# Attention of a hybrid layer on one core: the maxima row, the query copies, the first weights, the values and the last sums written in other places

## The chip, the cores and the metric

The kernel runs on one core of a Trainium2 chip. The metric is the device time of one execution in microseconds (us). A core has TensorE (PE in the profile, with its weight loads as PEld), VectorE (DVE), ScalarE (ACT), GpSimd (POOL) and SyncE (SP). SP computes nothing here: it issues most DMA transfers, strictly in its own order, and POOL issues some too.

## The reference, cut to what matters

One layer: a combined input projection feeds an RWKV-7 branch (A) and a latent attention branch (B), both are gated, projected, merged by sigmoid gates, projected again and added to the input. The change lies in branch B and at its two ends. Branch B computes, for 8 heads and 2048 tokens:

```
q = (rmsnorm(c_q, g_q) @ w_uq)       # per head 64 plain + 32 rotary
kv = (rmsnorm(c_kv, g_kv) @ w_ukv)   # per head 64 key + 64 value
q_pe = rope(q_pe, cos, sin);  k_pe = rope(k_pe, cos, sin)     # k_pe is shared by the heads
s = (q_nope . k_nope + q_pe . k_pe) * scale, masked to key <= query
p = softmax(s);  o = p @ v;  y_b = (o * silu(z_b)) @ w_out_b
```

## The kernel before

Every fp32 operand of a matrix product is split into a high and a low part, and a product is made as three matmuls (`mm3`). The time falls into three stretches. **Phase 1** (to about 1138 us) makes the input projections, the RWKV chunks, the values of the attention and, last, gate projections (tile `pj`) that are stored for the output phase (`d_zg`). Then comes a **seam**: the weights of the first pair of heads, its keys, the first queries. **Phase 2** (to about 1803 us) is the attention; **phase 3** makes the remaining gates, the output projections and the norm.

The attention works on pairs of heads (4 pairs `p`) and groups of 512 queries (4 groups `g`): 16 items, `i = 4p + g`. One item needs, in this order:

- `queries(i)`: two projections of six matmuls into one PSUM tile `pq`. Half k=0 holds the plain part, copied out as QH (ACT) and QL (DVE); half k=1 the rotary part, which DVE turns with the table `rt` (loaded by SP), splits as `qhl`, and which SP then copies by six DMAs of 64 KB into the tiles QR and QM.
- `row_max(i)`: for each 128 queries a tile `pm` of approximate scores, its maximum over the keys taken by DVE (`mx`, about 1.2 us for a full tile), then the negated maxima (`mh`), turned into a row by eight small matmuls (`pn`) and copied by ACT into row 32 of QM. That row is used in the fifth of the five products of a score tile, so that the exponential sees scores minus maximum.
- `attend(i)`: for each block `kb` of 128 keys a score tile `pst` (five products, each a pair of matmuls for the two heads), the exponential on ACT (`acc` for the first block, `pt` for the others), the value product into `po` and the sum of the exponentials on POOL (`acc`, 2 us a tile).

`pm`, `pq`, `pn`, `pst` and `bc` share one PSUM tag `st` with three buffers. The matmuls of the attention keep the order in which they are written; all other instructions are ordered by a scheduler. The written order comes from a list `steps`: before an item starts, its own maxima and the queries of the next item must be done (`due`); as far as that allows, `slot` puts one step between score tiles. Where an item is due and its steps are not done, they stand in a row, and I call that a forced start. At the end `total` sums `acc` over the partitions (`psum_s`), and `norm` spreads the reciprocals (`bc`) over the outputs. After that phase 3 begins with gate projections `pj`, whose weights `whl` and inputs `xh`, `xl` are loaded during the last items.

At the seam, `attn_weights(0)` loads nine small pieces of weights behind the last stores on SP (kraw and wqraw), `keys` makes pk in two halves, and the rotary keys are loaded once for all items by six transfers of 256 KB on POOL (tiles KR4 and KR5, named KR in the profile).

Of the kernel before, what the change touches and what calls it, by code (L numbers as in the profile page):

```python
# [19 lines left out]
P = 128  # L20
# [29 lines left out]
def hybrid_layer(ctx, tc, x, positions, g_pre, w_in, b_gate, mu_shift, w0, w_decay_up, a0, w_iclr_up, k_k, k_a,  # L50
# [234 lines left out]
    def proj(ps, w, X, cut=1):  # L285

        XH, XL = X
        for i in range(cut):
            t = slice(i * 512 // cut, (i + 1) * 512 // cut)
            mm3(ps[:, t], [(w[c], (XH[:, c, t], XL[:, c, t])) for c in range(KC)])  # L290


    with st:
# [590 lines left out]
        def attn_weights(p, pool, bufs):  # L884

            kraw = pool.tile([P, 2, HD], F32, name="kraw", tag="kraw", bufs=1)
# [3 lines left out]
            split(kwh, kwl, kraw.rearrange("p h n -> p (h n)"), A, V)  # L890
# [3 lines left out]
            for pieces in ([(HD * h, HD, hq[h][:, 0:HD]) for h in range(2)],  # L894
# [3 lines left out]
                qws[p].append(load_w(pool, None, 2, P, bufs=bufs, tag="wq", pieces=pieces))  # L898
# [5 lines left out]
        split(vh, vl, vraw, A, V)  # L904
        run(step(NH))
        for t in range(NT):
            ps = pp.tile([P, 512], F32, name="pv2", **(dict(tag="z", bufs=2) if t % 3 else dict(tag="e", bufs=1)))
            ts_ = slice(t * P, (t + 1) * P)
            mm3(ps, [((kvl[:, 0, ts_], kvl[:, 1, ts_]), (vh, vl))])
# [8 lines left out]
        sw = kst.enter_context(tc.tile_pool(name="pw", bufs=1, reuse_waits="tile", side="right"))  # L918
        attn_weights(0, sw, 2)
# [6 lines left out]
        def keys(p, psp, ptag, pbufs, mm):  # L926

            kwh, kwl = kws[p]
            for s in range(0, NS, 2):
# [6 lines left out]
                yield  # L936

# [17 lines left out]
        def queries(i, Q, sb, psp, ptag, pbufs, cqt=None, rt=None, mm=PE.matmul):  # L955
# [21 lines left out]
            split(hl[:, 0], hl[:, 1], ra, A, V)  # L977
            for h in range(2):
# [6 lines left out]
        def row_max(i, Q, KR4, sb, psp, ptag, pbufs, mm=PE.matmul):  # L985
# [5 lines left out]
            for j in range(4):  # L991
                js = slice(j * P, (j + 1) * P)
                for c in range(g + 1):
# [13 lines left out]
                    yield  # L1007
# [3 lines left out]
            V.tensor_scalar(mh, m1, -1.0, None, op0=ALU.mult)  # L1011
            pn = psp.tile([P, 2, 512], F32, name="pn", tag=ptag, bufs=pbufs)
            for h in range(2):
                for j in range(4):
                    mm(pn[0:1, h, j * P:(j + 1) * P], lhsT=mh[:, h, j:j + 1], rhs=identr, start=True, stop=True)
            for h in range(2):
                A.copy(QM[HD * h + 32:HD * h + 33, :], pn[0:1, h, :])
            yield
# [14 lines left out]
    with ExitStack() as st:  # L1033
# [3 lines left out]

        KR4 = sb.tile([P, T], F32R, name="KR4")
# [314 lines left out]
```

## Time and profile before

| what | us |
|---|---|
| median of three runs | 2496.98 (2496.0 to 2503.67) |
| the profiled execution | 2498.47 |
| its span in the trace | 2496.7 |
| PE busy | 2245.2 (90% of the span) |
| DVE busy | 1096.9 (44%) |
| ACT busy | 709.5 (28%) |
| POOL busy | 1018.5 (41%) |
| mean granted clock of TensorE | 0.945 |

A granted clock of 1.00 is 2.4 GHz, 0.50 is 1.2 GHz. The share of PE is an average: it is full during most of phases 1 and 3, some 87% in the attention and 41% at the seam. At the lower clock a matmul counts as busy for twice as long, so the busy share and the granted clock are read together.

### The profile page before, as it was taken

How to read it: one execution, taken by the hardware profiler on the slowest of the kernel's cores; microseconds unless marked ns; L12 is line 12 of the kernel's file. 1: busy time of each engine (PE TensorE's matmuls, PEld its weight loads, DVE VectorE, ACT ScalarE, POOL GpSimd, SP SyncE). 2: the span in 40 equal slices, each digit the busy share in tenths (PEclk: the TensorE clock that was granted, in tenths of full speed). 3: DMA queues.
4: the chain of work that ended last, by engine and by line, in shares of the span. 5: the costliest groups of instructions: out<-in, count | busy, mean ns of one | idle time of the engine just before them, and what ended most of it. 6: DMA issues, size and time to landing. Idle time of an engine off the chain costs nothing.

```text
span 2496.7 us, 37813 instructions
## 1 busy us (share of the span) xinstructions
PE 2245.2 (90%) x14313; PEld 1689.0 (68%) x14313; DVE 1096.9 (44%) x2005; ACT 709.5 (28%) x1267; POOL 1018.5 (41%) x1200
## 2 busy tenths in 40 slices
PE   7979998998999999894788989887799989999997
PEld 5656776777777777673565555554488867788776
DVE  7154785757677675422444534344130142310312
ACT  4342342333243432221233333322222211111111
POOL 7453542444275653211235654544522222312422
PEclk9989999989999999897889999999899999999999
DMA  7787766746577876745111112050197795765863
GB/s 249 217 270 231 238 218 182 204 118 210 168 222 203 259 200 228 205 136 148 55 57 56 49 56 73 28 186 7 52 358 235 268 333 208 278 211 195 322 236 118
DMA packets 314031, 454.75 MB, mean 182 GB/s; under 512 B 113661, under 2 KB 206905, under 8 KB 308025
## 3 DMA queue, kind: packets, MB, share of 16 engines
q1 hardware_dynamic: 283672, 404.09, 50.4%
q0 software_dynamic: 12896, 44.04, 5.5%
q10 hardware_dynamic: 17280, 4.20, 1.0%
q8 instruction: 113, 1.85, 0.3%
q14 instruction: 70, 0.57, 0.1%
HBM read 313.30 MB, written 132.64 MB: 179 GB/s over the span
## 4 chain that ended last, share of the span: by engine, by line
PE 64%; DVE 14%; DMA 12%; POOL 4%; issue 2%; ACT 2%; SPq 1%; ACTq 0%; POOLq 0%; DVEq 0%
PE pj L281 8%; PE pj L283 8%; PE pj L282 8%; PE pst L1066 7%; PE po L1066 5%; DMA wraw<-in_w_in_dram 3%; PE pm L1066 3%; PE pz L618 3%; DVE mx L1006 2%; DMA whl<-d_wi 2%; DVE Xg L673 2%; PE pout L281 2%; PE py L281 2%; PE pout L282 2%; PE py L283 2%
## 5 line engine op out<-in xcount | busy, mean ns | idle before, releaser
L281 PE MATMUL pj<-xh,whl 128*128 128x512 f32 (+2 forms) x1344 | 540.9, 402 | 39.0 <-DMA whl<-d_wi 26.6
L283 PE MATMUL pj<-xh,whl 128*128 128x512 f32 (+2 forms) x1344 | 537.9, 400 | 5.6 <-POOL whl L248 5.5
L282 PE MATMUL pj<-xl,whl 128*128 128x512 f32 (+2 forms) x1344 | 536.1, 399 | 0.0
L1120 POOL TENSOR_TENSOR acc<-acc,pt 128x1024 f32<-128x1024 f32 (+2 forms) x144 | 290.3, 2016 | 240.9 <-ACT pt L1107 113.8
L281 PEld LDWEIGHTS pj<-xh,whl 128*128 128x128 f32 (+1 forms) x1344 | 258.8, 193 | 105.7 <-DMA whl<-d_wi 27.3
L283 PEld LDWEIGHTS pj<-xh,whl 128*128 128x128 f32 (+1 forms) x1344 | 258.6, 192 | 69.0 <-POOL whl L248 10.8
L282 PEld LDWEIGHTS pj<-xl,whl 128*128 128x128 f32 (+1 forms) x1344 | 258.4, 192 | 55.5 <-issue 2.1
L1006 DVE TENSOR_REDUCE mx<-pm 128x2 f32<-128x1024 f32 (+3 forms) x160 | 166.7, 1062 | 215.9 <-PE pm L1066 215.3
L248 POOL TENSOR_TENSOR whl<-wraw,whl 128x512 fp32r<-128x512 f32 (+1 forms) x114 | 148.4, 1304 | 166.8 <-ACT whl L247 147.7
L1278 DVE SCALAR_TENSOR_TENSOR tg<-tg,py 128x512 f32<-128x512 f32 x64 | 43.9, 687 | 313.3 <-PE py L283 217.6
L1107 ACT ACTIVATE pt<-pst 128x1024 f32<-128x1024 f32 (+2 forms) x144 | 126.9, 883 | 187.7 <-PE pst L1066 177.7
L1280 POOL TENSOR_TENSOR tg<-tg 128x512 f32<-128x512 f32 x32 | 41.3, 1290 | 211.5 <-DVE tg L1278 211.5
L247 ACT CAST whl<-wraw 128x512 fp32r<-128x512 f32 (+1 forms) x116 | 71.4, 615 | 187.0 <-DMA wraw<-in_w_in_dram 99.1
L1066 PE MATMUL po<-pt,Vt 128*64 128x512 f32 (+3 forms) x576 | 122.3, 542 | 0.0
L281 PE MATMUL py<-BH,whl 128*128 128x512 f32 x256 | 102.5, 401 | 10.0 <-DVE tg L1278 9.9
L282 PE MATMUL py<-BL,whl 128*128 128x512 f32 x256 | 102.0, 399 | 0.0
L283 PE MATMUL py<-BH,whl 128*128 128x512 f32 x256 | 102.0, 398 | 0.0
L282 PE MATMUL pout<-wf,MH 128*128 128x512 f32 x256 | 101.0, 395 | 0.0
L283 PE MATMUL pout<-wf,ML 128*128 128x512 f32 x256 | 99.5, 395 | 0.0
L281 PE MATMUL pout<-wf,MH 128*128 128x512 f32 x256 | 97.2, 395 | 0.5 <-DMA wf<-d_wf 0.5
L671 DVE TENSOR_TENSOR tq<-Xg,Qg 128x30 f32<-128x30 f32 (+7 forms) x240 | 77.5, 323 | 44.6 <-DMA Xg<-d_q 39.1
L740 POOL TENSOR_TENSOR sp<-uv,pcs 64x256 f32<-64x256 f32 x64 | 41.1, 643 | 118.6 <-DVE uv L754 115.9
(372 smaller groups left out, 4044.1 us busy)
## 6 DMA issues: line engine op xcount, KB each, us to landing
whl<-d_wi SPq DMA_DIRECT2D x222, 512.0 KB
d_wi<-whl SPq DMA_DIRECT2D x80, 512.0 KB
wraw<-in_w_in_dram SPq DMA_DIRECT2D x98, 256.0 KB
whl<-d_wo SPq DMA_DIRECT2D x48, 512.0 KB
wf<-d_wf SPq DMA_DIRECT2D x48, 512.0 KB
cqt<-d_cq POOLq DMA_DIRECT2D x16, 1024.0 KB, 5.3
d_zg<-thg SPq DMA_DIRECT2D x42, 256.0 KB
xl<-d_x POOLq DMA_DIRECT2D x8, 1024.0 KB, 10.3
```

What stands on the lines that cost most here:

```text
L247: (ehi.copy if ehi is A else ehi.tensor_copy)(hi, src)
L248: elo.tensor_tensor(lo, src, f32(hi), op=ALU.subtract)
L281: mm(ps, lhsT=lh, rhs=rh, start=(i == 0), stop=False)
L282: mm(ps, lhsT=lh, rhs=rl, start=False, stop=False)
L283: mm(ps, lhsT=ll, rhs=rh, start=False, stop=(stop and i == n - 1))
L618: PE.matmul(pz[:, p, :], lhsT=E["BK"][p][b, c, :], rhs=E["AR"][b, p, c, :], start=True, stop=True)
L671: V.tensor_tensor(t3, Xg[:, 0:m, s_:s_ + 1].to_broadcast([P, m, n]), Qg[:, s_:s_ + 1, s_ + 1:32].to_broadcast([P, m, n]), op=ALU.mult)
L673: V.tensor_tensor(Xg[:, 0:m, s_ + 1:32], Xg[:, 0:m, s_ + 1:32], t3, op=ALU.add)
L1006: V.tensor_reduce(mx[:, :, j, c], pm[:, :, 0:w], axis=AX.X, op=ALU.max)
L1066: tc.keep_in_program_order(PE.matmul(*args, **kw))
L1107: A.activation(pt[:, :, q0:512], pst[:, :, q0:512], AF.Exp, scale=scale)
L1120: G.tensor_tensor(acc[:, :, q0:512], acc[:, :, q0:512], pt[:, :, q0:512], op=ALU.add)
```

## The change

It has six parts:

1. `attn_weights(0)` is written ahead of the last RWKV step, in memory that is free by then, and all attention weights go through one raw buffer (`raws=1`, tag wqraw shared with kraw).
2. The 16 value tiles (48 matmuls) are no longer written before the stored gates, but between the first keys, the first query projection and the first maxima, with their matmuls kept in written order.
3. The rotary keys are loaded by `rot_keys` in transfers of 64 KB on SP: first 512 tokens into a tile of its own for item 0 (6 transfers), then the whole for all other items (24 transfers).
4. `queries` projects the rotary half first (k = 1, then 0); rope and its split stand ahead of the copies QH and QL, and PE projects both halves without a stop.
5. `row_max` ends with `mh`. The row `pn` is made by `max_row` inside `attend`, after the first four products of the item's first two score tiles; the fifth products follow. The queries of the next item stand four maxima steps before the end of the list instead of three, and the first two blocks of an item have one slot for steps instead of three.
6. Three of the gate projections of phase 3 (`pj2`, 24 matmuls each) are written between the last sums.

```diff
         split(vh, vl, vraw, A, V)
+        sw = kst.enter_context(tc.tile_pool(name="pw", bufs=1, reuse_waits="tile", side="right"))
+        attn_weights(0, sw, 2)
         run(step(NH))
-        for t in range(NT):
+        def value(t):
...
+            mm3(ps, [((kvl[:, 0, ts_], kvl[:, 1, ts_]), (vh, vl))], mm=pin)
...
+        def rot_keys(pool, n):
+            K4 = pool.tile([P, n * 512], F32R, name="KR4")
+            K5 = pool.tile([P, n * 512], F32R, name="KR5")
+            for s in range(n):
+                ss_ = slice(s * 512, (s + 1) * 512)
+                for r in range(4):
+                    nc.sync.dma_start(f32(K4[32 * r:32 * r + 32, ss_]), f32(d_kr[:, 0, ss_]))
+                for h in range(2):
+                    nc.sync.dma_start(f32(K5[HD * h:HD * h + 32, ss_]), f32(d_kr[:, 1, ss_]))
...
-            for k in range(2):
-                ps = pq[:, k, :]
-                mm3(ps, [(qws[p][k][c], (cqt[:, c, 0, :], cqt[:, c, 1, :])) for c in range(2)], mm=mm)
-                if k == 0:
-                    split(QH, QL, ps, A, V)
+            for k in (1, 0):
+                mm3(pq[:, k, :], [(qws[p][k][c], (cqt[:, c, 0, :], cqt[:, c, 1, :])) for c in range(2)], mm=mm)
+            ps = pq[:, 1, :]
...
             split(hl[:, 0], hl[:, 1], ra, A, V)
+            split(QH, QL, pq[:, 0, :], A, V)
...
+        KR0 = rot_keys(sq, 1)
         with tc.tile_pool(name="pks", bufs=1, reuse_waits="tile", space=PSUM) as ppk:
-            for _ in queries(0, Q0, sq, ppk, "pk", 1, load_cq(0, sq), load_rt(0, sq)):
-                pass
+            t = 0
+            for _ in queries(0, Q0, sq, ppk, "pk", 1, load_cq(0, sq), load_rt(0, sq), mm=pin):
+                for t in range(t, t + 3):
+                    value(t)
+                t += 1
+            for _ in row_max(0, Q0, KR0[0], sq, ppk, "pk", 1, mm=pin):
+                for t in range(t, min(t + 2, NT)):
+                    value(t)
+                t += 1
...
-        KR4 = sb.tile([P, T], F32R, name="KR4")
-        KR5 = sb.tile([P, T], F32R, name="KR5")
-        for r in range(4):
-            G.dma_start(KR4[32 * r:32 * r + 32, :], d_kr[:, 0, :])
...
+        KR4, KR5 = rot_keys(sb, NS)
...
+                    for sc in two:
+                        next(sc)
+                    max_row(i, Q[i % NQ] if i else Q0, pp, "st", 3)
+                    flush(0)
+                    for sc in two:
+                        next(sc)
+                    slot(0)
...
-            at_ = max(0, len(steps) - 3)
+            at_ = max(0, len(steps) - 4)
...
-        while after:
-            follow()
+        for p in range(4):
+            if p < 3:
+                ps = pp.tile([P, 2, 512], F32, name="pj2", tag="st", bufs=3)[:, 0]
+                proj(ps, load_w(sx, w_in[:, C_ZA + p * P:C_ZA + (p + 1) * P], KC, P, elo=V, bufs=5,
+                                key=f"i{C_ZA + p * P}"), X, mm=pin)
...
+            for _ in range(1 if p < 3 else len(after)):
+                follow()
```

What this makes of the order of instructions is shown at three places. The first is the seam on SP. Before, behind the last gate store (d_zg) stand the weights and three tables; the rotary keys are on POOL's queue and not here:

```order
L492 DMA d_zg_17_401<-thg 128x512
L887 DMA kraw<-in_w_ukv_dram 128x2x64
L269 DMA wqraw<-in_w_uq_dram 128x2x64 x2
L269 DMA wqraw<-in_w_uq_dram 128x2x32
L269 DMA wqraw<-in_w_uq_dram 128x2x16 x2
L269 DMA wqraw<-in_w_uq_dram 128x2x32
L269 DMA wqraw<-in_w_uq_dram 128x2x16 x2
L945 DMA rt<-d_rope 128x512 x3
```

Now the weights are gone from here; the six copies of item 0's queries (QRx, QMx) are followed by the 24 loads of the whole rotary keys (KR_11905 and KR_11906; three more rounds of six are left out), and only then by the tables rt of items 1 and 2 and the query copies of item 1 (QR_11939). The first of the 24 loads writes memory that phase 1 held, and waits for the last value matmul:

```order
L1000 DMA QRx<-qhl 32x512
L1001 DMA QRx<-qhl 32x512
L1002 DMA QMx<-qhl 32x512
L951 DMA KR_11905<-d_kr 32x512 x4
L953 DMA KR_11906<-d_kr 32x512 x2
...
L966 DMA rt<-d_rope 128x512 x2
L891 DMA kraw<-in_w_ukv_dram 128x2x64
L966 DMA rt<-d_rope 128x512
L1000 DMA QR_11939<-qhl 32x512
```

The 24 loads moved from POOL to SP and stand between item 0's query copies and everything of item 1.

The second place is a forced start on PE, that of item 10. Before, two maxima tiles (pm) stand between the query projections (pq, twelve matmuls) and the row pn, and all five products of a score tile (pst) behind it:

```order
L1066 MATMUL pq<-cqt,wqhl 128x512 x12
L1066 MATMUL pm<-KH_11778,QH_11864 128x512 x2
L1066 MATMUL pm<-KR_11850,QR_11866 128x512 x2
L1066 MATMUL pm<-KH_11778,QH_11864 128x512 x2
L1066 MATMUL pm<-KR_11850,QR_11866 128x512 x2
L1066 MATMUL pm<-ident_9773,nmask_9772 128x128 x4
L1066 MATMUL pn<-identr,mh 1x128 x8
L1066 MATMUL pst<-QH_11864,KH_11778 128x512 x2
```

Now four maxima tiles follow pq (the last of them is shown), then eight pairs of score products (the last two are shown), then pn, two value products of the item before, and the two fifth products:

```order
L294 MATMUL pm<-KH_11682,QH_11937 128x512 x2
L294 MATMUL pm<-KR_11905,QR_11939 128x512 x2
L294 MATMUL pm<-ident_9773,nmask_9772 128x128 x4
...
L294 MATMUL pst<-QH_11937,KL_11683 128x512 x2
L294 MATMUL pst<-QR_11939,KR_11905 128x512 x2
L294 MATMUL pn<-identr,mh 1x128 x8
L294 MATMUL po<-pt,Vt_9806 64x256 x2
L294 MATMUL po<-pt,Vt_9806 64x128 x2
L294 MATMUL pst<-QM_11940,KR_11906 128x512 x4
```

The row pn moved behind two more maxima tiles and eight pairs of products, and the fifth products moved behind ACT's copies of pn.

The third place is the end of the attention on PE. Before, the last sums (psum_s) and the spread reciprocals (bc) follow the last value product directly:

```order
L1066 MATMUL po<-pt,Vt_9807 64x128 x2
L1066 MATMUL psum_s<-acc,osel 64x512 x2
L1066 MATMUL bc_16981<-rhl,bsel 128x512 x2
L1066 MATMUL bc_16988<-rhl,bsel 128x512 x2
L281 MATMUL pj_17012<-xh_15844,whl 128x512
```

Now one projection stands ahead of psum_s and two between psum_s and bc (the ends of the first and the second are shown, and the start of the third):

```order
L294 MATMUL pj_16998<-xl_15862,whl 128x512
L294 MATMUL pj_16998<-xh_15861,whl 128x512
L294 MATMUL psum_s<-acc,osel 64x512 x2
L294 MATMUL pj_17041<-xh_15861,whl 128x512
...
L294 MATMUL pj_17041<-xh_15861,whl 128x512
L294 MATMUL pj_17073<-xh_15861,whl 128x512
```

Both waits at the end now have 24 and 48 matmuls ahead of them.

## Rows read from the trace of the kernel before

**Rows 1.** Stretches: busy time of PE, PEld, DVE, ACT, POOL, PEclk, DMA, GB/s

```profile
1050.00:1137.00 87.00, 85.84 (x683) 68.15 (x677) 16.91 (x43) 24.19 (x49) 7.88 (x12) 0.96 0.45 140
1137.00:1205.00 68.00, 27.90 (x128) 20.20 (x128) 18.93 (x25) 9.53 (x17) 12.83 (x35) 0.62 0.46 119
1205.00:1760.00 555.00, 483.05 (x3514) 305.99 (x3513) 243.40 (x289) 181.94 (x235) 270.31 (x151) 0.94 0.19 61
```

**Rows 2.** Waits of PE, 1137 to 1205: us in total, times, longest

```profile
PE pk L281 <- ACT kwh L247: 16.6, 1, 16.6
PE pm L1066 <- DMA QR<-qhl: 7.3, 1, 7.3
```

**Rows 3.** Waits of PE in the attention, 1203 to 1760

```profile
PE pn L1066 <- DVE mh L1011: 38.9, 14, 4.4
PE pq L1066 <- DVE QL L248: 20.0, 14, 1.6
PE pm L1066 <- DVE mx L1006: 8.3, 18, 1.7
```

**Rows 4.** Chain that ends the seam, pieces by start: start us, us, what

```profile
1138.66 7.81 DMA d_zg<-thg
1146.53 7.21 DMA kraw<-in_w_ukv_dram
...
1176.44 2.02 DMA QRx<-qhl
...
1195.42 3.86 DMA QR<-qhl
```

**Rows 5.** Forced start of item 10 on PE: start, us, instruction [idle before]

```profile
1535.26 1.65 PE L1066 MATMUL pq<-cqt,wqhl 128*128 128x512 f32 x6 [1.40 <-DVE QL L248]
...
1537.17 0.39 PE L1066 MATMUL pm<-KR,QR 64*128 64x512 f32 x2
1537.40 0.40 PE L1066 MATMUL pm<-KH,QH 64*128 64x512 f32 x2
...
1542.64 1.01 PE L1066 MATMUL pn<-identr,mh 128*1 128x128 f32 x8 [4.43 <-DVE mh L1011]
...
1544.17 0.63 PE L1066 MATMUL pst<-QL,KH 64*128 64x512 f32 x2
1544.60 0.63 PE L1066 MATMUL pst<-QH,KL 64*128 64x512 f32 x2
```

**Rows 6.** The same start on DVE

```profile
1534.51 0.69 DVE L248 TENSOR_TENSOR QL<-pq,QH 128x512 fp32r<-128x512 f32 x1 [0.62 <-ACT QH L247]
1536.95 0.68 DVE L973 TENSOR_TENSOR qra<-pq,rt 64x512 f32<-64x512 f32 x1 [1.74 <-PE pq L1066]
...
1538.41 1.23 DVE L1006 TENSOR_REDUCE mx<-pm 128x2 f32<-128x1024 f32 x1
...
1542.32 0.17 DVE L1011 TENSOR_SCALAR mh<-m 128x8 fp32r<-128x8 f32 x1
```

**Rows 7.** The same start on ACT

```profile
1543.26 1.17 ACT L1017 CAST QM<-pn 1x512 fp32r<-1x512 f32 x2 [2.26 <-PE pn L1066]
```

**Rows 8.** Stretches of 10 us in the attention, columns of the first group

```profile
1440.00:1450.00 10.00, 5.58 (x35) 4.16 (x35) 5.39 (x8) 1.77 (x3) 0.58 (x1) 0.76 0.56 170
1540.00:1550.00 10.00, 7.36 (x48) 5.48 (x50) 2.43 (x5) 4.29 (x6) 0.00 (x0) 0.66 0.40 134
1690.00:1700.00 10.00, 7.35 (x44) 4.58 (x44) 7.86 (x9) 0.59 (x1) 0.00 (x0) 1.00 0.00 0
1740.00:1750.00 10.00, 5.32 (x41) 2.94 (x38) 9.38 (x11) 0.00 (x0) 0.00 (x0) 0.95 0.00 0
```

**Rows 9.** SP's queue at the seam: start, us of issue, DMA

```profile
1176.44 0.58 SPq L981 DMA_DIRECT2D QRx<-qhl  x1
1194.18 0.51 SPq L980 DMA_DIRECT2D QR<-qhl  x1
```

**Rows 10.** DMA issues, 1137 to 1215: queue, count, KB, median us to landing

```profile
KR<-d_kr POOLq DMA_DIRECT2D x6, 256.0 KB, 8.4
```

**Rows 11.** End of the attention on PE

```profile
1793.38 1.97 PE L1066 MATMUL psum_s<-acc,osel 128*64 128x512 f32 x4 [5.59 <-POOL acc L1120]
1800.37 2.04 PE L1066 MATMUL bc<-rhl,bsel 128*128 128x512 f32 x4 [5.02 <-DVE rhl L1143]
1802.94 0.80 PE L281 MATMUL pj<-xh,whl 128*128 128x512 f32 x1 [0.53 <-DVE Ou L1152]
...
1805.24 0.63 PE L283 MATMUL pj<-xh,whl 128*128 128x512 f32 x1
1805.67 0.63 PE L281 MATMUL pj<-xh,whl 128*128 128x512 f32 x1
```

More of the change, by code (lines that the diff above doesn't have):

```diff
@@ L289, in proj, with pin @@
             t = slice(i * 512 // cut, (i + 1) * 512 // cut)
-            mm3(ps[:, t], [(w[c], (XH[:, c, t], XL[:, c, t])) for c in range(KC)])
+            mm3(ps[:, t], [(w[c], (XH[:, c, t], XL[:, c, t])) for c in range(KC)], mm=mm)
+    def pin(*args, **kw):
+        tc.keep_in_program_order(PE.matmul(*args, **kw))
     with st:
@@ L889, in attn_weights @@
             kwl = pool.tile([P, P], F32R, name="kwl", tag="kwl", bufs=1)
-            split(kwh, kwl, kraw.rearrange("p h n -> p (h n)"), A, V)
+            split(kwh.rearrange("p (h n) -> p h n", h=2), kwl.rearrange("p (h n) -> p h n", h=2), kraw, A, V)
             kws[p], qws[p] = (kwh, kwl), []
@@ L936, in keys @@
                 yield
+        def rot_keys(pool, n):
[7 more added lines that the diff above has]
+                    nc.sync.dma_start(f32(K5[HD * h:HD * h + 32, ss_]), f32(d_kr[:, 1, ss_]))
+            for h in range(2):
+                V.memset(f32(K5[HD * h + 32:HD * h + 33, :]), 1.0)
+            return K4, K5
         def load_cq(g, pool):
@@ L1024, in hybrid_layer @@
         Q0 = q_tiles(sq, "x")
+        KR0 = rot_keys(sq, 1)
         with tc.tile_pool(name="pks", bufs=1, reuse_waits="tile", space=PSUM) as ppk:
-            for _ in queries(0, Q0, sq, ppk, "pk", 1, load_cq(0, sq), load_rt(0, sq)):
-                pass
+            t = 0
[7 more added lines that the diff above has]
+                t += 1
+            for t in range(t, NT):
+                value(t)
     first.close()
@@ L1060, in hybrid_layer @@
             G.memset(rsgn[32 * k:32 * k + 32], -1.0 * (k % 2))
-        pair, late, after = {}, [], []
-        def mm(*args, **kw):
-            tc.keep_in_program_order(PE.matmul(*args, **kw))
+        pair, late, after, gates0 = {}, [], [], []
         def flush(n):
@@ L1091, in scores @@
                 diag = kb >= 4 * g
-                for k, (kt, qt, n) in enumerate(((kh, QH, HD), (kh, QL, HD), (kl, QH, HD), (KR4, QR, HD),
-                                                 (KR5, QM, 33))):
+                for k, (kt, qt, n) in enumerate(((kh, QH, HD), (kh, QL, HD), (kl, QH, HD), (k4, QR, HD),
+                                                 (k5, QM, 33))):
+                    if k == 4:
+                        yield
                     for h in range(2):
                         r = slice(h * HD, h * HD + n)
-                        mm(pst[:, h, q0:512], lhsT=kt[r, ks_], rhs=qt[r, q0:512], start=(k == 0),
-                           stop=(k == 4 and not diag))
+                        pin(pst[:, h, q0:512], lhsT=kt[r, ks_], rhs=qt[r, q0:512], start=(k == 0),
+                            stop=(k == 4 and not diag))
                 if diag:
@@ L1100, in scores @@
                         for h in range(2):
[L1101 to L1102 removed]
+                            pin(pst[:, h, q0:q0 + P], lhsT=ident2[HR[h], a, :], rhs=nmask2[HR[h], a, :],
+                                start=False, stop=(a == 1))
                 if kb == 0:
```

72 lines of the change are left out of this document (39 added, 33 removed).

## The prediction

> **What bounds the kernel now.** I read the stretches first. Up to the seam TensorE is full: 85.84 of the last 87 us of phase 1. In the 68 us of the seam it works 27.90, at a granted clock of 0.62; in the attention 483.05 of 555, at 0.94 [rows 1]. So the change can win only at the seam, in the 72 us of idle time and the lost clock of the attention, and in the waits at its end. Next the waits. At the seam PE stands 16.6 us for the split weights kwh and later 7.3 us for item 1's query copies QR [rows 2]. The chain shows what the first is made of: the store of the last gate lands 7.81 us after its issue, and only then does the weight load start, 7.21 us; the queries' own copies land in 2.02 and 3.86 us [rows 4]. In the attention nearly all idle time has two names: pn waits for mh (14 times, 38.9 us) and the second query projection for the copy QL (14 times, 20.0 us) [rows 3]. The forced start of item 10 shows both: 1.40 us before the second half of pq, 4.43 us before pn, and then score matmuls 0.43 us apart (1544.17 to 1544.60), where a pair takes 0.23 at the full clock (1537.17 to 1537.40) [rows 5]. In that stretch the granted clock is 0.66 on average, so part of it ran at the lower level; 1690 to 1700, with 7.35 us of work, kept 1.00 [rows 8].
>
> **Seam, what goes.** The weights are loaded before the last RWKV step, so the 16.6 us go. The 48 value matmuls leave a stretch where PE is full (48 x 0.23 = 11.0 us) for one where it idles: keys and queries wait there for copies, and the values fill those waits. So 11.0 us are won if they stay covered; if the cover is gone they cost 11.0 again, or 22 at half the clock. The 7.3 us wait for QR goes into a new one, below. PE no longer starts the keys after a long pause; of the 27.90 us of work at clock 0.62 (some 10 us lost) I give back 4. Together 16.6 + 11.0 + 7.3 + 4 = 39 us.
>
> **Seam, what comes.** First, DVE's first key copy KL now stands behind the last rows of the RWKV output, which wait for a store and a load; before, 37 projections hid that. The nearest landings are 2.02 and 7.81 us [rows 4], which bounds the sum of two by 4 and 16; three values cover 2.1 of it, and I take 7. Second, the 24 loads of KR. They wait for the last value matmul and stand on SP ahead of the table rt that item 1's rope needs. SP takes 0.51 to 0.58 us for a 64 KB transfer [rows 9], so the table is issued 12 to 14 us late and lands 2.0 to 8.4 us after that (a query copy, and the 256 KB rotary loads of before [rows 4, 10]). Behind it stand three rope steps (0.68 to 0.71 each) and the query copies before pq gives its PSUM buffer to pn, about 4.3. So pn comes 18.5 to 26.7 us after the last value, while PE has 12 matmuls and 8 pairs, 4.6 us: 14 to 22 us idle. I take 16, near the low end, because the table is one transfer with nothing behind it. Third, the second pair's weights, now through one raw buffer: two casts on ACT stand between the exponentials of item 0 and wait for loads that SP issues behind item 1's copies. Bounds 0 and 2 x 7.21 [rows 4]; I take 7, one landing. Together 30, so the seam wins **9**. By the bounds it goes from 20 lost (9, 6 and 7 more for the three, and 7 of the values' cover) to 21 won (3, 2 and 7 less).
>
> The Trainium skill speaks to the second point from both sides. "DMA: Bandwidth & Descriptors", section "Issuing engines are not separate DMA queues", says that the engine that starts a transfer matters only by its sequencer time, usually small beside the transfer; by that the move from POOL to SP would cost next to nothing and the seam would win 25. Here the row prices that sequencer time at 0.51 to 0.58 us, 24 times over. The table "Rules for kernel authors" on the same page advises joining small transfers, and this change cuts six into 24.
>
> **Attention.** Take the forced start of item 10 from the end of pq (time 0). DVE has to do, in the order of the changed program: qra 0.68, product 0.71, a maximum 1.23, sum 0.69, two maxima 2.46, low part 0.67, QL 0.69, the last maximum 1.23, m and mh 0.33 [rows 6]: 8.7 us. PE has four pm (0.93 each) and eight score pairs (1.85): 5.6 us. With three PSUM buffers the third pm waits for the first maximum (0.9 us), the fourth for the second (1.0), the first score tile for the third (0.3), the second for QL (0.45) and pn for mh (0.8): 3.4 us, in pieces of at most 1.0. New is the wait of the fifth products for ACT's two copies of pn, 1.17 us [rows 7], of which the rest of pn and a short value product cover some 0.3: 0.9. So 4.3 us instead of 5.83, a factor of 0.74. Over 14 starts, 58.9 us become 43.6: **15** won. Bounds: nothing, where the short starts gain a copy wait and lose none; 30, if mh is done in time in half of them.
>
> The clock comes on top. 555 x (1 - 0.94) = 33 us of full clock are missing in the attention [rows 1]. In item 10's start 10 x 0.34 = 3.4 us are missing, of which 2.4 fell on work and the rest on idle time, so some 23 us of work time hang on the clock. The pieces of idle time are now 1 us instead of 4.4, and pauses of 1.4 us for QL stand in the trace without a lower clock behind them. I take two thirds, **16**, with bounds 0 and 23.
>
> **End.** psum_s waits 5.59 us for POOL's last sum, bc 5.02 for the reciprocals, pj 0.53 [rows 11]: 11.1 us. One projection (24 x 0.23 = 5.5) covers the first, two (11.0) the second. The work moves, none is added. Around the waits psum_s and bc took 1.97 and 2.04 us at the low clock, about half of it too much, and the first nine pj came 0.43 apart instead of 0.23 (1805.24 to 1805.67), 1.8: together 3.8. So **15**, if the weights for three projections are there in time; lower bound 8, where phase 3's own waits for loads take some of it back.
>
> **Sum.** 9 + 15 + 16 + 15 = 55 us from the profiled execution: 2498.47 - 55 = 2443 (span 2441.7 and 1.8 around it). The median before is 1.5 lower than that execution, which I leave as noise.
>
> **Rivals.**
> 1. The KR loads hide. If the 24 transfers go out early enough, or the table arrives ahead of them, the 16 us and the 6 us behind them in item 1 are not lost, and the clock in item 0 stays up: 2443 - 16 - 6 - 7 = **2414**. For it: item 0 needs none of them, and the DMA engines were busy only 0.46 of the seam [rows 1]. Against: SP issues in order.
> 2. The clock does not come back (0 of 16): **2459**; with the KR landings at 8.4 us, eight in flight, 3 x 8.4 = 25 instead of 13 us, 12 more and 5 for what follows: **2476**. For it: 1440 to 1450 fell to 0.76 with 5.58 us of work.
> 3. Slower: every start now has many small waits in a stretch of some 14 us with 9.4 us of work (12 pq 2.8, four pm 3.7, ten pairs 2.3, pn 0.6), and if the clock falls to its lower level at each and stays there, that work takes 9.4 us longer, of which the 4.3 us of waits absorb their part: 5.1 a start, against 1.6 now (23 over 14). 15 x 3.5 = 53 lost instead of 16 won: 2443 + 16 + 53 = **2512**. It decides from about 4.2 us lost to the clock a start: 15 x (4.2 - 1.6) is the 39 won elsewhere. For it: such mixed stretches at the seam ran at 0.62. Against: 1740 to 1750, with 5.32 us of work in small pieces behind DVE, kept 0.95 [rows 8]. In the Trainium skill, "TensorE: Matmul & The Clock Gate", section "What's actually happening", has it that the low clock is the default state and activity releases it; that would favour this rival, and the row at 0.95 does not bear it out.
> 4. No change that can be measured: the seam loses 20, no clock comes back, the end pays 8: 2498.5 + 20 - 15 - 8 = **2496**.
>
> **How the numbers follow.** The forecast, 2443, with a band of 2425 to 2465, gets 0.50; rival 1 0.15; rival 2 0.20; rival 3 0.08; rival 4 0.07. A difference of 0.3% (7.5 us) is about what a measurement of this kernel can tell from none. Faster: 0.50 + 0.15 + 0.20 = 0.85; same 0.07; slower 0.08. The range takes in rivals 1 and 2 with some room, 2408 to 2482, and leaves 3 and 4 out.
>
> **What would show it.** In the changed profile: no wait of pk for kwh; the values between the keys; a wait of 14 to 22 us before the first pn with SP busy on KR just before; no wait of pq for QL; waits of pn for mh below 1.5 us and a new one of pst for the QM copies of about 0.9; fewer 10 us stretches below 0.9; no gap at the end. The prediction is wrong if the KR loads leave no gap, if the clock falls at most starts, or if phase 3 starts earlier without ending earlier.

## The result and the profile after

The changed kernel takes 2462.43 us (median of four, 2461.81 to 2464.45) against 2496.49 us before: ratio 0.9869, 95% interval 0.9851 to 0.9886. That is 34 us faster where 55 were forecast. The profiled execution took 2461.92 us, with a span of 2459.8 and a mean granted clock of 0.954. All ratios are taken from fast runs; one run of part1_back below, at 5290.19 us, is left out of its ratio and range.

Four marks on TensorE divide both spans: the end of the last stored gate projection, the first matmul of item 2's query projection, the end of the last value product, and the end of the span.

| stretch | before, us | after, us | won | forecast |
|---|---|---|---|---|
| phase 1, to the last gate | 1137.9 | 1127.6 | 10.3 | 11 |
| seam, to item 2's queries | 72.2 | 78.4 | -6.2 | -2 |
| attention, to the last value product | 577.7 | 559.4 | 18.3 | 31 |
| the rest | 708.9 | 694.4 | 14.5 | 15 |

The forecast's 9 for the seam is the sum of its first two lines, 11 - 2, where the runs gave 4. Each stretch is read from one execution, so a line of this table is less sure than the whole; how far a stretch scatters stands ahead of the experiments. The rows of the attention between the marks, of before and then of after (us, then busy time of PE, PEld, DVE, ACT, POOL, granted clock, DMA share, GB/s):

```profile
1210.10:1787.80 577.70, 505.74 (x3658) 317.48 (x3656) 239.39 (x285) 191.60 (x244) 296.86 (x162) 0.94 0.19 58
```

```profile
1206.00:1765.30 559.30, 510.01 (x3671) 314.66 (x3669) 237.39 (x287) 188.15 (x244) 296.11 (x162) 0.96 0.19 61
```

Idle time fell from 72.0 to 49.3 us, but busy time rose by 4.3, with 13 matmuls more in the stretch. The waits of PE in the attention of after answer to [rows 3] (us in total, times, longest):

```profile
PE pm L294 <- DVE mx L1026: 35.0, 45, 1.7
PE pn L294 <- DVE mh L1032: 5.3, 7, 2.9
PE pm L294 <- DVE QL L248: 3.4, 4, 1.4
...
PE pst L294 <- ACT QM L1046: 0.4, 1, 0.4
```

The two waits of before are gone under their names: pn waits 5.3 us for mh instead of 38.9, though in pieces of up to 2.9 where the forecast had them below 1.5, and pq for QL not at all. Most of what is left stands before maxima tiles, in 45 pieces of at most 1.7 us. The new wait for the copies QM is 0.4 us in the whole attention.

The seam of after on PE (start, us, instruction, idle time before), to be read beside [rows 2]:

```profile
1128.43 0.73 PE L294 MATMUL pk<-kvl,kwh 128*128 128x512 f32 x2 [0.83 <-ACT thg L495]
...
1129.92 2.26 PE L294 MATMUL pv<-vtmp,kvl 128*128 128x512 f32 x9
1141.54 1.22 PE L294 MATMUL pk<-kvl,kwh 128*128 128x512 f32 x2 [9.36 <-DVE KL L248]
...
1167.92 0.97 PE L294 MATMUL pv<-vtmp,kvl 128*128 128x512 f32 x3
1168.73 2.97 PE L294 MATMUL pq<-cqt,wqhl 128*128 128x512 f32 x12
...
1190.04 1.01 PE L294 MATMUL pn<-identr,mh 128*1 128x128 f32 x8 [14.95 <-DVE QL L248]
```

The 16.6 us for kwh are gone, but 9.36 us for KL stand right behind the first keys and 14.95 us before the first pn. DVE in that first gap:

```profile
1126.95 0.88 DVE L793 SCALAR_TENSOR_TENSOR bvb<-ypt,prm,bvb 128x256 f32<-128x256 f32 x2 [5.37 <-PE ypt L789]
...
1139.44 0.88 DVE L793 SCALAR_TENSOR_TENSOR bvb<-ypt,prm,bvb 128x256 f32<-128x256 f32 x2 [10.34 <-DMA KR<-d_kr]
1140.26 1.23 DVE L248 TENSOR_TENSOR KL<-pk,KH 128x1024 fp32r<-128x1024 f32 x1
```

DVE stands before the last two rows of the RWKV output, and KL queues behind them. The releaser named is KR, the load that landed nearest to that time; the rows' own input bvb goes out on SP between two stores of d_ya, ahead of KR's first four:

```profile
1129.24 1.18 SPq L792 DMA_DIRECT2D bvb<-d_ya  x2
1130.59 2.19 SPq L951 DMA_DIRECT2D KR<-d_kr  x4
```

DVE starts 9 us after the issue of bvb. In the same time KR's loads and two loads of 1 MB by POOL are under way, the second of them for item 1's queries:

```profile
1129.41 0.54 POOL L961 DMA_DIRECT2D cqt<-d_cq  x1
```

SP in the second gap (start, us of issue), and what DVE waits for there:

```profile
1168.92 1.70 SPq L951 DMA_DIRECT2D KR<-d_kr  x4
...
1182.26 0.90 SPq L966 DMA_DIRECT2D rt<-d_rope  x2
```

```profile
1185.65 0.68 DVE L992 TENSOR_TENSOR qra<-pq,rt 64x512 f32<-64x512 f32 x1 [11.31 <-DMA rt<-d_rope]
```

The 24 loads begin with the end of the last value matmul (1168.9) and the table rt goes out 13.3 us later. DVE's first rope step of item 1 waits 11.31 us for it, and PE's 14.95 us before pn end with the copies behind that step. The end of the attention answers to [rows 11]:

```profile
1771.06 1.08 PE L294 MATMUL psum_s<-acc,osel 128*64 128x512 f32 x4
1783.09 1.09 PE L294 MATMUL bc<-rhl,bsel 128*128 128x512 f32 x4
1785.69 0.50 PE L281 MATMUL pj<-xh,whl 128*128 128x512 f32 x1 [1.51 <-DVE th L1265]
```

No wait is left before psum_s and bc, and both run at the full clock.

### The profile page after: what moved, and what is told of

The parts are those of the page before. It is cut to its first block, busy times and chain, and to the rows that moved or that the text cites. A ratio compares the mean times of both kernels' runs of the same rounds, so it can differ in the third digit from the quotient of the medians.

```text
span 2459.8 us, 37864 instructions
## 1 busy us (share of the span) xinstructions
PE 2245.5 (91%) x14313; PEld 1682.1 (68%) x14313; DVE 1092.0 (44%) x2007; ACT 704.9 (29%) x1267; POOL 1018.1 (41%) x1194
## 4 chain that ended last, share of the span: by engine, by line
PE 58%; DVE 16%; DMA 15%; POOL 4%; issue 4%; ACT 2%; SPq 2%; ACTq 0%; DVEq 0%; POOLq 0%
PE pj L281 7%; PE pst L294 7%; PE pj L283 7%; PE pj L282 7%; PE po L294 5%; DVE mx L1026 3%; DMA whl<-d_wi 3%; DMA wraw<-in_w_in_dram 3%; PE pout L281 2%; PE pout L283 2%; PE pout L282 2%; PE pz L622 2%; DVE Xg L677 2%; PE py L281 2%; DVE tq L675 2%
## 5 line engine op out<-in xcount | busy, mean ns | idle before, releaser
L281 PE MATMUL pj<-xh,whl 128*128 128x512 f32 (+1 forms) x1320 | 530.8, 402 | 36.3 <-DMA whl<-d_wi 22.4
L283 PE MATMUL pj<-xh,whl 128*128 128x512 f32 (+1 forms) x1320 | 528.1, 400 | 5.2 <-POOL whl L248 5.1
L282 PE MATMUL pj<-xl,whl 128*128 128x512 f32 (+1 forms) x1320 | 525.5, 398 | 0.0
L281 PEld LDWEIGHTS pj<-xh,whl 128*128 128x128 f32 x1320 | 253.5, 192 | 101.2 <-DMA whl<-d_wi 21.1
L283 PEld LDWEIGHTS pj<-xh,whl 128*128 128x128 f32 x1320 | 253.4, 192 | 67.3 <-POOL whl L248 10.5
L282 PEld LDWEIGHTS pj<-xl,whl 128*128 128x128 f32 x1320 | 254.1, 192 | 54.3 <-issue 2.1
L294 PE MATMUL pm<-KH,QH 64*128 64x512 f32 (+3 forms) x312 | 71.0, 443 | 40.7 <-DVE mx L1026 35.0
L675 DVE TENSOR_TENSOR tq<-Xg,Qg 128x30 f32<-128x30 f32 (+7 forms) x240 | 77.8, 324 | 43.4 <-DMA Xg<-d_q 37.9
```

The source lines that it names most:

```text
L281: mm(ps, lhsT=lh, rhs=rh, start=(i == 0), stop=False)
L282: mm(ps, lhsT=lh, rhs=rl, start=False, stop=False)
L283: mm(ps, lhsT=ll, rhs=rh, start=False, stop=(stop and i == n - 1))
L294: tc.keep_in_program_order(PE.matmul(*args, **kw))
L675: V.tensor_tensor(t3, Xg[:, 0:m, s_:s_ + 1].to_broadcast([P, m, n]), Qg[:, s_:s_ + 1, s_ + 1:32].to_broadcast([P, m, n]), op=ALU.mult)
```

## The experiments

All start from the changed kernel unless said otherwise. The end of phase 1 moved between 1120 and 1134 us in kernels whose gates were written alike, so I compare stretches from one mark to the next in the profiled executions, beside the medians of the timed runs. "Seam" and "attention" are the stretches of the table above. How far they scatter can be read from kernels that are alike there: the seam took 74.2 to 78.4 us in maxrow_back, k_order, end_back, greedy and the changed kernel, the attention 556.7 to 560.1 in seven kernels, and the rest 694.4 to 703.9 in the twelve with the changed end.

**Rotary keys back on POOL (kr_pool).**

```diff
-        KR4, KR5 = rot_keys(sb, NS)
+        for r in range(4):
+            G.dma_start(KR4[32 * r:32 * r + 32, :], d_kr[:, 0, :])
+        for h in range(2):
+            G.dma_start(KR5[HD * h:HD * h + 32, :], d_kr[:, 1, :])
...
```

> The changed kernel with the 24 loads of the whole rotary keys taken from SP and issued by POOL as six of 256 KB, as before the change; the table rt of item 1 is then issued ahead of the last value matmul. Theory (SP's order makes the gap): the wait of 14.95 us before the first pn falls to 0 to 4 us, and the time falls by 10 to 15 us, to 2448 to 2452. Rival (the amount of data makes it: 1.5 MB must land behind the last value matmul, and item 1's maxima wait for it): the gap moves to item 1's first maxima, and the time falls by 5 us at most.

Measured: 2457.51 us (2454.03 to 2465.73), ratio to before 0.9839 (0.9814 to 0.9863); seam 72.5, attention 556.9. The waits of PE at the seam:

```profile
PE pq L294 <- DMA cqt<-d_cq: 12.6, 1, 12.6
PE pk L294 <- DVE KL L248: 6.3, 1, 6.3
...
PE pn L294 <- DVE QL L248: 2.4, 1, 2.4
```

And the issues of SP and POOL:

```profile
1160.53 1.09 SPq L966 DMA_DIRECT2D rt<-d_rope  x2
1172.27 1.99 POOL L1078 DMA_DIRECT2D KR<-d_kr  x4 [37.40 <-PE pv L294]
...
1176.31 0.58 POOL L961 DMA_DIRECT2D cqt<-d_cq  x1
```

The wait before pn fell as the theory said: with the loads gone from SP, rt goes out 11 us before the last value matmul ends (1172.0). But 12.6 us came up before item 1's queries: KR now stands at the head of POOL's queue for 37.40 us until that matmul, and cqt, which the changed kernel had issued at 1129.41, goes out behind it. The gap moved and shrank by some 6, little more than the seam scatters, and the time fell by 5, within the intervals. Neither side is right: it is no matter of SP alone, but of the queue that holds the loads of KR.

**Item 1's inputs ahead of the rotary keys (kr_late).** kr_pool with

```diff
+        ahead = load_cq(1, sb), load_rt(1, sb)
         KR4 = sb.tile([P, T], F32R, name="KR4")
...
+            if cqt is None and i == 1:
+                cqt, rt = ahead
```

> As kr_pool (whole rotary keys on POOL as six transfers of 256 KB), with item 1's table rt and query input cqt loaded ahead of them. In kr_pool the gap had moved: pq of item 1 waited 12.6 us for cqt, which stood behind the six loads on POOL. Theory (the gap is made by the order of the queues, whichever engine's): with both ahead no wait over 5 us is left between the last value and the first pn, and the time falls by 8 to 13 us against the changed kernel, to 2449 to 2454. Rival (the 1.5 MB themselves take the time): a gap of 8 to 12 us stands before item 1's first maxima, whose keys then come last, and the time falls by 4 us at most.

Measured: 2463.62 us (2459.04 to 2466.18), ratio 0.9870 (0.9849 to 0.9891); seam 72.7, attention 557.0. The waits at the seam, and POOL's queue:

```profile
PE pq L294 <- DMA cqt<-d_cq: 9.3, 1, 9.3
PE pn L294 <- DVE QL L248: 7.0, 1, 7.0
PE pk L294 <- DVE KL L248: 6.4, 1, 6.4
```

```profile
1168.45 0.55 POOL L961 DMA_DIRECT2D cqt<-d_cq  x1 [37.62 <-PE pv L294]
```

and a wait on SP:

```profile
SPq L966 <- PE pv L294: 11.5, 1, 11.5
```

cqt is ahead of KR now and still waits 37.62 us for a value matmul, and on SP rt waits 11.5 for one. In the changed kernel cqt went out at 1129.41 and in kr_pool rt at 1160.53, both before the last value matmul. So this edit did more than change the order. Written ahead of KR, the two tiles seem to take the memory that KR's tiles had, which phase 1 holds until the last value; their addresses were not read. The theory therefore is not refuted: no run has the loads of KR waiting with nothing that is needed soon behind them in their queue. What kr_pool and kr_late show together is that a load into that memory waits for the last value on either engine, and what stands behind it in the queue waits too. The rival's gap before item 1's maxima did not come: no wait for keys stands there.

**The values before the gates again (values_back).**

```diff
+        for t in range(NT):
+            value(t)
         run(gates_seg())
...
             for _ in queries(0, Q0, sq, ppk, "pk", 1, load_cq(0, sq), load_rt(0, sq), mm=pin):
-                for t in range(t, t + 3):
-                    value(t)
+                pass
...
```

> The changed kernel with part 2 undone: the values before the stored gates again, all else as changed. Theory (the values cost nothing at the seam, as they fill its waits): the gates end 11 us later, the waits between the keys, the queries and the first maxima get longer by what the values covered, and the time rises by 5 to 11 us, to 2467 to 2473. Rival (at the seam they cost as much as before the gates, since copies of values stand on DVE before the splits of keys and queries): 0 to 3 us, or faster.

Measured: 2449.22 us (2447.38 to 2454.59), ratio 0.9818 (0.9797 to 0.9839), so 13 us faster than the changed kernel, where I expected 5 to 11 more. Seam 57.5, attention 556.7, last gate at 1131.3. The waits at the seam, and the first of the 24 loads and the table behind them on SP:

```profile
PE pm L294 <- DVE QLx L248: 8.1, 1, 8.1
PE pk L294 <- DVE KL L248: 6.9, 1, 6.9
...
PE pn L294 <- DVE QL L248: 2.6, 1, 2.6
```

```profile
1139.16 3.15 SPq L954 DMA_DIRECT2D KR<-d_kr  x4
...
1151.84 0.90 SPq L969 DMA_DIRECT2D rt<-d_rope  x2
```

Nothing of the second gap is left. The 24 loads stand on SP ahead of rt here as in the changed kernel, but they go out from 1139.16, 8 us behind the last gate, and rt is issued 30 us earlier than in the changed kernel. So the place on SP alone makes no gap; loads that wait for the last value do, with what stands behind them. The values' new place takes 21 us at the seam (78.4 against 57.5). What it gives back before the gates is 4 in this pair (1131.3 against 1127.6), within the scatter of that mark.

**The first weights behind the gates again (weights_back).**

```diff
-        sw = kst.enter_context(tc.tile_pool(name="pw", bufs=1, reuse_waits="tile", side="right"))
-        attn_weights(0, sw, 2)
         run(step(NH))
...
         NQ = 3
+        sw = kst.enter_context(tc.tile_pool(name="pw", bufs=1, reuse_waits="tile", side="right"))
+        attn_weights(0, sw, 2)
```

> The changed kernel with part 1 undone in its place only: attn_weights(0) written behind the gates again, still through one raw buffer. Theory (the 16.6 us wait for the first split weights is what part 1 takes away, and it comes back in full, with the wqraw pieces now one after another): the first pk waits 15 to 17 us for kwh, the wait for KL behind it shrinks as DVE's old work is done by then, and the time rises by 8 to 15 us, to 2470 to 2477. Rival (the wait for the last RWKV rows on DVE, 9.4 us, hides behind it, and the values' last matmul sets the seam): 0 to 5 us more.

Measured: 2458.08 us (2453.48 to 2462.80), ratio 0.9840 (0.9810 to 0.9871); seam 71.4, attention 559.0. pk did not wait for kwh. The order shows why: the scheduler put kraw among the gates although it is written behind them. So this run does not undo the part, and says only that the place in the text was not what held the weights back.

**Place and buffers of the first weights undone (part1_back).** As weights_back, and for the first pair

```diff
-            kraw = pool.tile([P, 2, P], F32, name="kraw", tag="wqraw", bufs=1)[:, :, 0:HD]
+            kraw = pool.tile([P, 2, P], F32, name="kraw", tag="wqraw" if p else "kraw", bufs=1)[:, :, 0:HD]
...
-                qws[p].append(load_w(pool, None, 2, P, bufs=bufs, tag="wq", pieces=pieces, raws=1))
+                qws[p].append(load_w(pool, None, 2, P, bufs=bufs, tag="wq", pieces=pieces, raws=1 if p else 2))
```

> The changed kernel with part 1 undone for the first pair in place and in buffers: attn_weights(0) behind the gates, kraw in a buffer of its own and two raw buffers. In weights_back, with the place alone undone, the scheduler still put the weight loads among the gates; with the larger memory they stand behind the last gate store again. Theory (the 16.6 us wait is what part 1 takes away): the first pk waits 14 to 17 us for kwh, the wait for KL behind it falls to 2 to 3 us as DVE's old rows are done meanwhile, and from the last gate to item 2's queries the kernel takes 8 to 11 us longer than the changed one (78.4); the time 2468 to 2474. Rival (the last value and the tables behind it set the seam whatever the weights do): no longer than 81 us, and the time within 3 us of 2462.

Measured: median 2462.75 us (2458.37 to 2464.45), ratio 0.9851 (0.9826 to 0.9875), with before at 2501.2 beside it; seam 75.8. The waits at the seam:

```profile
PE pn L294 <- DVE QL L248: 15.2, 1, 15.2
PE pk L294 <- ACT kwh L247: 9.3, 1, 9.3
```

The weights are late again, by 9.3 us, and the 9.4 us for KL are gone. The rival holds: in the changed kernel the early weights buy nothing that shows, since DVE still has the last RWKV rows ahead of the first key copy. Part 1 takes away one of two waits that lie over each other. Only 9.3 of the 16.6 us come back: the split of kraw starts 2.1 us after its issue (1132.39 to 1134.50), where the load alone took 7.21 before [rows 4]. Before, POOL had issued 3.5 MB in the 9 us ahead of that load, here 1 MB; that this is the reason is not tested.

**The maxima row back (maxrow_back).** Part 5 undone:

```diff
             mhs[i] = mh
+            max_row(i, Q, psp, ptag, pbufs)
             yield
...
-                    max_row(i, Q[i % NQ] if i else Q0, pp, "st", 3)
...
-            at_ = max(0, len(steps) - 4)
+            at_ = max(0, len(steps) - 3)
...
```

> The changed kernel with part 5 undone: pn again at the end of row_max, three slots in every block pair, queries three steps before the end. Theory (the move pays by splitting the waits and by the clock): waits of pn for mh are back at 35 to 55 us, pieces of over 3 us return, the granted clock of the attention falls, and the time rises by 15 to 25 us, to 2477 to 2487. Rival (DVE's work sets the length of a start wherever pn stands): idle time only changes its name, and the time rises by 0 to 6 us.

Measured: 2476.09 us (2471.19 to 2486.15), ratio 0.9923 (0.9892 to 0.9953), 14 us more than the changed kernel; attention 569.0. Its row, and two of its waits:

```profile
1202.60:1771.60 569.00, 506.87 (x3659) 321.19 (x3657) 240.32 (x285) 190.45 (x244) 297.00 (x162) 0.93 0.19 60
```

```profile
PE pn L294 <- DVE mh L1031: 42.1, 13, 5.0
PE pm L294 <- DVE mx L1026: 9.1, 17, 2.0
```

pn waits 42.1 us again, and the attention is 9.6 us longer. Idle time is 62.1 against 49.3, but busy time is 506.9 against 510.0 although the clock is 0.93 against 0.96. The time is 1 us below the range of the theory; its waits and its clock came. The three pieces of part 5 (the row, the slots, the earlier queries) were undone together, so this run does not divide the gain among them.

**The order of the query halves back (k_order).**

```diff
-            for k in (1, 0):
+            for k in range(2):
...
+                if k == 0:
+                    split(QH, QL, ps, A, V)
...
```

> The changed kernel with part 4 undone: the plain half of the queries projected and copied first. Theory: the second half of pq waits for QL again, 12 to 14 times 1.4 us, and as DVE stands still for part of that, a start gets longer by nearly as much: 12 to 20 us more, 2474 to 2482. Rival (DVE is the limit of a start and QL costs it 0.69 us in either place): 0 to 5 us more.

Measured: 2468.01 us (2464.92 to 2478.29), ratio 0.9892 (0.9863 to 0.9922); 5.6 us more than the changed kernel, with intervals that overlap; attention 568.9, 9.5 us longer, clear of its scatter. pq waits for QL 14 times, 22.3 us, but pm waits for mx only 21.0 us instead of 35.0. Between the two sides: somewhat more than half of the wait is only a change of name.

**The three projections back in phase 3 (end_back).** The loop over `p` behind the last `flush(0)` is replaced by the old two lines.

> The changed kernel with part 6 undone: the three gate projections stand in phase 3 again. Theory: two waits of about 5.5 and 5.0 us return at the end of the attention with some 3 us at half the clock, and the time rises by 11 to 15 us, to 2473 to 2477. Rival (phase 3 is paced by its loads and takes the gain back): 0 to 5 us more.

Measured: 2473.39 us (2471.79 to 2477.88), ratio 0.9910 (0.9887 to 0.9932), 11 us more; from the last value product to the end 705.8 instead of 694.4. psum_s waits 5.58 us and bc 5.02 again, and they take 1.97 and 2.04. The theory holds.

**A step in every slot (greedy).**

```diff
-            if done + spare < min(len(steps), 24 + (len(steps) - 24) * kbs // (10 * NG)):
+            if done + spare < len(steps):
```

> The changed kernel with the pacing of the steps taken away: every slot between two score tiles takes a step as soon as the due order allows it, so that only three starts are still forced and the maxima tiles stand between score tiles instead of in rows of 4 to 15. Theory (in the changed kernel the starts are as long as DVE's work in them, 8.7 us against 5.6 on PE, so only spreading that work takes idle time away): waits of pm for mx fall from 35 to under 15 us, pieces are shorter, the clock rises, and the time falls by 15 to 30 us, to 2432 to 2447. Rival (score tiles and maxima then compete for the three PSUM buffers, so that scores wait for maxima instead): the idle time of the attention stays within 10 us of 49, and the time within 7.

Measured: 2446.31 us (2443.22 to 2451.26), ratio 0.9805 (0.9783 to 0.9826), 16 us less than the changed kernel; attention 545.4, seam as before (78.4). The row of its attention and its waits:

```profile
1206.40:1751.80 545.40, 507.89 (x3671) 315.05 (x3669) 240.89 (x287) 189.66 (x244) 296.03 (x162) 0.95 0.19 62
```

```profile
PE pm L294 <- DVE mx L1026: 9.2, 9, 1.7
PE pn L294 <- DVE mh L1032: 9.1, 9, 2.9
PE pst L294 <- DVE QL L248: 6.5, 3, 2.2
PE pst L294 <- DVE mx L1026: 4.6, 8, 3.0
```

The maxima tiles stand between score tiles instead of in rows, and idle time is 37.5 us. That 12 of the 49 us were DVE's work crowded into the starts is shown; what the other 37.5 are made of was not tested. The clock did not rise (0.95), which was part of the expectation and failed.

**Combinations.** late_greedy is kr_late with greedy, vback_greedy is values_back with greedy; v9_late_greedy has seven values before the gates, nine between the keys and behind the first queries, and kr_late with greedy.

> kr_late and greedy together, as a version that may beat both kernels. Theory: the two act in different stretches and add up, 25 to 42 us below the changed kernel, 2420 to 2437. Rival (what greedy gains in the first items it only gains because the gap at the seam has put the maxima ahead): less than the larger of the two alone plus 3 us.

Measured: 2446.41 us (2434.32 to 2450.58), ratio 0.9808 (0.9788 to 0.9827): what greedy gives alone. Its seam is 72.1, as in kr_late, and its medians say that these 6 us of seam do not show in the time.

> values_back and greedy together: all values before the stored gates, and every slot takes a step. Theory (the values' new place is what holds back everything that is loaded into phase 1's memory, and greedy works in the attention, so they add up): 13 and 16 us below the changed kernel, 2430 to 2438. Rival (they gain in the same item starts): 2443 to 2449.

Measured: 2436.85 us (2426.82 to 2441.85), ratio 0.9750 (0.9720 to 0.9780); seam 60.9, attention 547.3. The two add up within some 4 us. This version beats both kernels: 60 us below before, 26 below the changed one.

> As vback_greedy, but nine of the sixteen values stand between the two key halves and behind the first queries, the last of them some 16 us earlier than in the changed kernel; the whole rotary keys are loaded by POOL behind item 1's cqt. Theory (values cost nothing where they fill a wait and where nothing needed soon waits for the last of them): no gap of over 4 us before the first pn, gates end 3 to 6 us earlier than in vback_greedy, and the time is 2 to 6 us below it. Rival (a value at the seam costs what it saved before the gates): equal to vback_greedy or slower.

Measured: 2439.31 us (2429.98 to 2441.89), ratio 0.9759 (0.9730 to 0.9787); seam 65.4. No gain over vback_greedy. Here item 0's maxima wait 9.4 us in one piece. The trace names wqraw, but that is issued later; item 0's copies QRx went out by 1156.9 and seem to land late, beside the 2.5 MB that POOL loads then. That is argued, not shown. The rival holds.

## Why the prediction was right, and where its steps failed

**The direction and most of the size held**, 34 us of 55, and each part of the sum can be set against a run. The whole came nearer than its parts, which is partly luck: the seam gave 4 where 9 were forecast, idle time in the attention 22.7 for 15, and its busy time rose by 4.3 where the clock was to shorten it by 16.

**End: right.** 15 forecast; 14.5 between the marks, 11 by end_back's median. The projections covered both waits, and the low clock went with them. The two waits are the surer evidence: the rest scatters by 9 us, and 694.4 is the lowest of its twelve.

**Seam, the weights: sizes near, cause wrong.** The 16.6 us wait did go, and 9.36 us for KL came where 7 were forecast. But I put the whole 16.6 down to the place of the weights. Both waits lie over the same stretch: part1_back has a wait for kwh of 9.3 and none for KL, the changed kernel 9.4 for KL and none for kwh. The gain of part 1 by itself is within what the runs can tell from nothing (seam 75.8 against 78.4, times alike), and the rest of the 16.6 went by what else was changed.

**Seam, the values: the gain was booked, the price was put down to the loads.** The prediction said that 11.0 us of values are won where they fill waits, and that they cost 11 again if the cover is gone. The values did fill waits, and phase 1 ended earlier; but values_back, which gives that gain up, is 13 us faster. The prediction had the link in its text ("They wait for the last value matmul") and charged the gap that follows from it to the place of the KR loads on SP, not to the values that hold those loads back.

**Seam, the gap before pn: the chain and the size right, one half of the cause left out.** 14 to 22 us were forecast, 16 taken, 14.95 measured. The chain came as written: KR waits for the last value, rt stands behind it on SP and goes out 13.3 us late where I had 12 to 14, and rope, copies and pn wait for rt. The 13.3 are made up otherwise: four issues took 1.70 us, so 0.42 each instead of 0.51 to 0.58, and the rest are pauses. The gap needs both the held memory and the queue. With KR on POOL the wait before pn is 2.4, but POOL's cqt stands behind KR (kr_pool); with the values earlier the gap is gone although all 24 loads are on SP ahead of rt (values_back). On this the Trainium skill, "DMA: Bandwidth & Descriptors", section "Issuing engines are not separate DMA queues", says that another issuing engine saves only its sequencer time, usually small beside the transfer. The trace agrees in part: moving the loads to POOL shortened the seam by some 6 us, not by 16, but the 13.3 us for which the 24 loads held SP are not small.

**Seam, the two smaller terms.** The casts of the second pair's weights were booked at 7 us. ACT waits 5.6 us for their loads, but PE waits only 0.86 and 1.37 us for the exponentials behind them. The 4 us of clock did not come: 21.4 us of the seam's work ran at the lower level before and 24.1 after.

**Attention, idle time: right in kind, too small.** 15 forecast, 22.7 measured. The forced start of item 10 had 5.83 us of waits and was given 4.3. In the changed kernel its rows from pq to the fifth products are:

```profile
1523.77 3.06 PE L294 MATMUL pq<-cqt,wqhl 128*128 128x512 f32 x12
1529.41 0.49 PE L294 MATMUL pm<-KH,QH 64*128 64x512 f32 x2 [1.34 <-DVE mx L1026]
...
1531.39 0.50 PE L294 MATMUL pm<-KH,QH 64*128 64x512 f32 x2 [1.25 <-DVE mx L1026]
...
1532.52 0.79 PE L294 MATMUL pst<-QH,KH 64*128 64x512 f32 x2 [0.22 <-DVE mx L1026]
...
1535.98 0.64 PE L294 MATMUL pn<-identr,mh 128*1 128x128 f32 x8
```

That is 2.8 us. The forecast's 0.45 and 0.8 before the second score tile and pn, and its 0.9 for QM, are not there: the pauses before the third and fourth maxima tiles are longer (1.34 and 1.25 for 0.9 and 1.0) and give DVE time enough, most of the eight score pairs ran at the lower clock from 1532.52, and two value products and the rest of pn cover ACT's copies. k_order and maxrow_back each give back 9.5 us of the attention, together 19 of the 18.3 won.

**Attention, the clock: the term that failed in size.** 16 us were forecast and about 5 came, hidden under other work. The granted clock did rise, 0.94 to 0.96. In the stretches where the traces give it as 0.50, TensorE was busy for 55.0 us before and 43.4 after. At 0.43 us for a pair of matmuls instead of 0.23 [rows 5], that is 25.6 and 20.2 us lost, an estimate. The clock still fell, close to 8 of the 15 starts of items 1 to 15, where before it fell close to 11. Item 10 is one of the 8 (columns of [rows 8]):

```profile
1530.00:1540.00 10.00, 8.53 (x62) 6.24 (x62) 5.11 (x8) 5.04 (x9) 0.72 (x1) 0.83 0.51 147
```

That meets by the letter one sign of being wrong that the prediction names, a clock that falls at most starts. Busy time rose all the same, by 4.3 us. Two more maxima tiles lie between the marks (12 matmuls, some 1.2 us). maxrow_back has 3 us less of busy time than the changed kernel, though 64.5 us of it ran at the lower clock. The mean of a matmul in the attention hardly moved (mean ns behind the comma), before and then after:

```profile
L1066 PE MATMUL pst<-QL,KH 64*128 64x512 f32 (+2 forms) x312 | 63.1, 389 | 0.0
L1066 PE MATMUL pst<-QM,KR 33*128 33x512 f32 (+2 forms) x312 | 61.7, 381 | 0.0
```

```profile
L294 PE MATMUL pst<-QL,KH 64*128 64x512 f32 (+2 forms) x312 | 61.5, 382 | 0.0
L294 PE MATMUL pst<-QM,KR 33*128 33x512 f32 (+2 forms) x312 | 62.9, 381 | 0.5 <-ACT QM L1046 0.4
```

The step that failed is the belief that shorter pauses bring back two thirds of the work lost to the clock: the loss itself was near (25.6 for 23), but about a fifth came back. Why the work at the full clock grew by some 10 us, so that nothing of it shows, stays open; that each pause adds the start and the tail of a matmul to busy time would fit with more pauses (45 before maxima tiles against 18), but no run tests it.

**The rivals.** Rival 1 did not come in the changed kernel. values_back makes its condition true, loads that go out early enough, and gains 13 us where the rival had 29. Rival 2, no clock, is near to what happened to that term, and its 2459 lies 3 us from the result; that it is so close is luck, as other terms missed in both directions. Rival 3 did not come: no start ran at the lower clock throughout. Rival 4 did not come: phase 1 and the seam together won 4 us where it had 20 lost, and the end paid 14.5, not 8.

## What to carry to other kernels

When work is moved later to fill a gap, ask what is released by its last instruction, and what stands in the queues behind a load that waits for it: here 11 us of matmuls in a gap held a memory region, the loads into it held a queue, and the seam was 21 us longer. Two waits that follow each other in the trace of before may hide a third under the first, so a wait that is taken away is worth only what it is longer than the next wait under it. And where an engine that feeds the bound is short only in some places (DVE at the item starts), spreading its work over the others can win more than reordering the starts: one line of pacing gave 16 us here.

## What the runs showed of the hardware that was not expected

Two things. One load that cannot go yet holds its queue on either engine: KR's first load stood 37.40 us at the head of POOL's queue in kr_pool, with cqt behind it, and 11.5 us at the head of SP's in the changed kernel, with rt behind it. And pauses that are short do not keep the granted clock up by themselves: in the changed kernel 1530 to 1540, with pauses of 1.34, 1.25 and 0.22 us in it and just before it and 8.53 us of work, had 0.83, where [rows 8] show 0.66 behind a pause of 4.43 [rows 5]. Over the whole attention that made 0.96 with 45 waits of up to 1.7 us before maxima tiles, against 0.94.
